# Transposing the residual unnormalised during the output projection, with the first two query blocks and six gate chunks moved

## The chip, the cores and the metric

The kernel runs on one core of a Trainium2 chip. The metric is the device time of one execution in microseconds (us), as a median of several runs. One core has TensorE (PE, matmuls; PEld is its weight load), VectorE (DVE), ScalarE (ACT), GpSimd (POOL) and SyncE (SP), which work in parallel, each in the order of its own queue. In this program SP issues nearly all large loads, and POOL the small transfers and the stores.

## The reference

One decoder layer on 256 tokens of width 2048, all in float32: a modulated norm, an input projection, sparse attention and retention side by side, an output projection with a gated residual, a second modulated norm, and a retrieval of experts (PEER) with a gated residual.

```python
mod = (c_act @ w_ada[l] + b_ada[l]).reshape(B, 6, 1, D)
shift1, scale1, gate1, shift2, scale2, gate2 = jnp.moveaxis(mod, 1, 0)
...
x = x + gate1 * (jnp.concatenate([o_nsa, o_ret], axis=-1) @ w_out[l])
h2 = rmsnorm(x, g_norm_ffn[l]) * (1.0 + scale2) + shift2
x = x + gate2 * peer_ffn(h2, peer_w_q[l], peer_sub_keys[l], peer_u[l], peer_v[l])
return rmsnorm(x, g_norm_final)
```

In `peer_ffn`, `q = h2 @ w_q` gives 8 heads x 2 halves of 128 numbers per token, that is 16 query blocks of 128 columns. Each is scored against 128 keys, the best 16 of each half are paired, and the best 16 of the pairs are the experts. Each token then needs `gelu(h2 . u)` and a sum of rows of `v` for its experts only.

## The kernel before, in words

Weights come in chunks of 128x2048 numbers, 1 MB each. `load` (L146) issues one on SP into a slot `raw`. `split_to` (L153) makes two reduced-precision halves of it: ACT casts the high part (`whi`, L157), and VectorE subtracts it from the original for the low part (`wlo`, L158). A product is then three matmuls (high x high, high x low, low x high). The activations stand likewise as `hh` and `hl`, the two halves of the tile `act`.

**The six modulation vectors** are 6 x 16 chunks of `adaT`. `ada_chunk` (L195) loads one and multiplies it by the row of c on VectorE with a running sum (L198). `background(pace)` (L327) interleaves them with other work from the list `todo`: at each call it adds `PACE[pace]` to a credit and takes as many chunks as the credit has whole numbers. Vector 5 is gate 2; it is needed only at the end of the program. Six of its 16 chunks stand at the end of `todo` (`LATE = 6`), ten are done in the query stage.

**Output projection.** `n_tile(q, "woutN", ...)` (L442) is called for four column blocks q, each with four chunks of weights and 96 matmuls into `psN`. Its result is multiplied by gate 1 (`xg`, L716) and added to the residual `x2` (L717). ACT sums the squares (L719), and POOL stores `x2` (L720). `x2` and `xT` are two views of the same memory.

**The turn.** When the last block is done, the reciprocal root-mean-square `rc` of each token is taken (L723), `x2` is multiplied by it (`xn`, L728), 32 transposes go into `psX` (L733), ACT and VectorE by turns add scale and shift into `xT` (L737 and L739), ACT casts `hh` (L740) and VectorE makes `hl` (L741).

**Query stage.** A second pool of slots opens (five `raw`, three `whi`, two `wlo`), over memory of the front. First come the loads of the keys (`skT`) and of the first two weight chunks `wqT`. `t_blocks` (L227) makes the first two query blocks side by side: for each of 16 steps k and each block a matmul of 128x512 with the high weights on both halves of `act` (L236) and one of 128x256 with the low weights on `hh` (L237). Fourteen single blocks follow. Each block is summed into `pq` (ACT L245, VectorE L246), scored (`pss`, L1089), and its top 16 are found on VectorE (L1071 to L1075); block 2 is split into a tile `pair` of its own, so that its split can be done early. In the first ten rounds an `ada_chunk` of gate 2 is done with `crow2`, a copy of the row of c that POOL loads (L1133). From the scores come candidates, the picks and the indices for gathers.

**Activation and value halves.** `u_half` (L1238) goes through 64 chunks of `u`, each 16 matmuls into `psU` (L1062); beside it one-hot matrices `pg` mark the experts. `v_group` multiplies with the chunks of `v`. The order is u half 0, v group 0, u half 1, v group 1. In u half 1 the chunks use slots of `raw` and three of `whi`, one after another in a ring (`set_ring`, L129). Before u half 0, gate 2 is finished into a row (`row5`, L1272 to L1279).

What sets the order: a scheduler places the instructions of each engine by program order and by `tc.high_priority`; loads wait for the slot that they reuse.

Of the kernel before, what the change touches and what calls it, by code (L numbers as in the profile page):

```python
# [30 lines left out]
PACE = dict(A=2, C=0.5, B=0.8, pair=1.5, tile=1.4, head=1.4, out=0.75)  # L31
LATE = 6
# [83 lines left out]
def body(ctx, tc, a, out, dbg=None, stop=None):  # L116
# [110 lines left out]
    def t_blocks(pool, src_chunks, tags=("A", "A"), parts=1, dst=None):  # L227

        if dst:
            split_to(load(src_chunks[0]), *dst, parts)  # L230
        w = [dst] if dst else [split(load(c), parts=parts) for c in src_chunks]
        ps = [pool.tile([P, 2, S], F32, name="psA", tag=t) for _, t in zip(w, tags)]
        for k in range(KB):
            sl = slice(k * P, (k + 1) * P)
            for p_, (hi, lo) in zip(ps, w):
                nc.tensor.matmul(p_, hi[:, sl], act[:, k], start=k == 0, stop=False, skip_group_check=True)  # L236
                nc.tensor.matmul(p_[:, 1, :], lo[:, sl], hh[:, k, :], start=False, stop=k == KB - 1, skip_group_check=True)  # L237
        return ps

    def t_block(pool, src_chunk, tag="A", **kw):  # L240
        return t_blocks(pool, [src_chunk], (tag,), **kw)[0]
# [36 lines left out]
    with ExitStack() as fctx:  # L278
# [43 lines left out]

        todo = [(j, k) for k in range(KB) for j in (1, 0)] + [(j, k) for j in (2, 4, 3) for k in range(KB)] + [(5, k) for k in range(LATE)]

# [68 lines left out]
        for k in range(KB):  # L393
# [3 lines left out]
            if len(todo) > 46 + LATE:  # L397
                background("B")
# [322 lines left out]
        xn = fp.tile([P, 2, D], F32, name="xn", tag="oT")  # L721
        with tc.high_priority(offset=100):
            rc = token_rstd(fp, ss, 2, "rc")  # L723
        for q in range(4):
            sl = slice(q * 512, (q + 1) * 512)
            with tc.high_priority(offset=(4 - q) * 40):
                for tt in range(2):
                    nc.vector.tensor_scalar(xn[:, tt, sl], x2[:, tt, sl], rc[:, tt:tt + 1], None, op0=OP.mult)  # L728
        for k in range(KB):
            with tc.high_priority(offset=(KB - k) * 10):  # L730
                ps = pp.tile([P, 2, P], F32, name="psX", tag="TO"[k % 2])
                for tt in range(2):
                    nc.tensor.transpose(ps[:, tt, :], xn[:, tt, k * P:(k + 1) * P], ident)  # L733
                t = xT[:, k, :]
                ps = ps.rearrange("p t s -> p (t s)")
                if k % 2:
                    nc.vector.tensor_scalar(t, ps, scol[:, 1, k:k + 1], modc[:, 3, k:k + 1], op0=OP.mult, op1=OP.add)  # L737
                else:
                    nc.scalar.activation(t, ps, AF.Identity, bias=modc[:, 3, k:k + 1], scale=scol[:, 1, k:k + 1])  # L739
                nc.scalar.copy(hh[:, k, :], t)  # L740
                nc.vector.tensor_sub(hl[:, k, :], t, hh[:, k, :].bitcast(F32))  # L741


    with ExitStack() as gctx:
# [338 lines left out]
        wq = lambda i: a["wqT"][i].rearrange("p k e -> p (k e)")  # L1083
# [188 lines left out]
        nc.vector.tensor_add(modc[:, 5, :], modc[:, 5, :], b_col[:, 5, :])  # L1272
        nc.vector.tensor_scalar(modc[:, 5, :], modc[:, 5, :], 1.0 / GSC, None, op0=OP.mult)
        ps = up.tile([P, 512], F32, name="psh", tag=bank("S"))
        nc.tensor.transpose(ps[0:KB, 0:P], modc[:, 5, :], ident)
        r5 = gp_.tile([KB, P], F32, name="row5t", tag="ge", bufs=3)
        nc.scalar.copy(r5, ps[0:KB, 0:P])
        row5 = dram.tile([1, D], F32, name="row5")
        nc.gpsimd.dma_start(row5.rearrange("o (k p) -> (o k) p", p=P), r5)  # L1279
# [36 lines left out]
```

## Time and profile before

| | |
|---|---|
| median of 3 runs | 1909.55 us (1908.13 to 1912.08) |
| profiled execution | 1904.08 us |
| span of its trace | 1902.3 us |
| mean granted TensorE clock | 0.982 |
| bytes moved | 652.91 MB, mean 343 GB/s |

The span reaches from the first to the last instruction; 1.8 us of the profiled execution lie around it. Times in rows are microseconds from the start of the span, "mean ns" is that of one instruction. A matmul's time is pipelined: successive ones overlap, so the distance of their starts is the better measure. "x16" in a row stands for 16 instructions. In brackets or after the last bar stands the time that the engine was idle just before, and what ended it. Names are those of the program: `psN` and `psA` are PSUM tiles of the output projection and of the query blocks, and a row "psN L452 <- DVE wlo L158" is a wait of TensorE for a split.

### The profile page before, as it was taken

How to read it: one execution, taken by the hardware profiler on the slowest of the kernel's cores; microseconds unless marked ns; L12 is line 12 of the kernel's file. 1: busy time of each engine (PE TensorE's matmuls, PEld its weight loads, DVE VectorE, ACT ScalarE, POOL GpSimd, SP SyncE). 2: the span in 40 equal slices, each digit the busy share in tenths (PEclk: the TensorE clock that was granted, in tenths of full speed). 3: DMA queues.
4: the chain of work that ended last, by engine and by line, in shares of the span. 5: the costliest groups of instructions: out<-in, count | busy, mean ns of one | idle time of the engine just before them, and what ended most of it. 6: DMA issues, size and time to landing. Idle time of an engine off the chain costs nothing.

```text
span 1902.3 us, 28433 instructions
## 1 busy us (share of the span) xinstructions
PE 1811.7 (95%) x11303; PEld 1585.4 (83%) x11303; DVE 1477.1 (78%) x2247; ACT 697.5 (37%) x1191; POOL 370.8 (19%) x256
## 2 busy tenths in 40 slices
PE   5899899999988999999999999999999999999995
PEld 3799878798776899999997777779999997777773
DVE  7878887889768999677478999984455567888875
ACT  3344453545425421021035555541111114555542
POOL 1000000012000012211124333331111114544210
PEclk9999999999998999999999999999999999999998
DMA  8989888989778879989989999989999989999981
GB/s 337 371 314 351 319 331 245 346 280 345 265 258 343 297 284 361 425 351 360 373 327 378 420 413 414 414 322 426 365 361 368 351 318 391 404 387 387 384 298 44
DMA packets 94471, 652.91 MB, mean 343 GB/s; under 512 B 11409, under 2 KB 11617, under 8 KB 18433
## 3 DMA queue, kind: packets, MB, share of 16 engines
q1 hardware_dynamic: 66818, 467.78, 64.8%
q0 software_dynamic: 27520, 183.32, 24.2%
q8 instruction: 89, 1.46, 0.3%
q14 instruction: 44, 0.36, 0.1%
HBM read 644.97 MB, written 4.22 MB: 341 GB/s over the span
## 4 chain that ended last, share of the span: by engine, by line
PE 72%; DVE 12%; DMA 11%; issue 3%; ACT 1%; POOL 0%; SPq 0%; ACTq 0%; POOLq 0%; DVEq 0%
PE acc L964 31%; PE psU L1062 25%; DMA raw<-in_adaT 7%; PE psN L452 5%; DVE wlo L158 3%; PE psA L236 2%; PE psD L353 2%; DVE raw L198 2%; DMA raw<-in_winB 1%; PE bkC L353 1%; PE psA L237 1%; PE pg L1047 1%; ACT whi L157 1%; DMA raw<-in_winA 1%; DVE s L844 1%
## 5 line engine op out<-in xcount | busy, mean ns | idle before, releaser
L1062 PE MATMUL psU<-xT,raw 128*128 128x160 f32 x4096 | 571.1, 301 | 4.0 <-ACT ge L1067 2.5
L1062 PEld LDWEIGHTS psU<-xT,raw 128*128 128x128 f32 x4096 | 559.9, 191 | 5.0 <-ACT ge L1067 2.6
L964 PE MATMUL acc<-whi,cc 128*128 128x512 f32 x1512 | 367.8, 391 | 0.0
L947 DVE TENSOR_TENSOR wlo<-raw,whi 128x2048 fp32r<-128x2048 f32 x126 | 288.3, 2288 | 72.3 <-issue 59.3
L964 PEld LDWEIGHTS acc<-whi,cc 128*128 128x128 f32 x1512 | 283.9, 188 | 68.8 <-issue 0.2
L964 PE MATMUL acc<-wlo,cc 128*128 128x512 f32 x1008 | 254.2, 393 | 2.4 <-DVE wlo L947 2.4
L198 DVE SCALAR_TENSOR_TENSOR raw<-raw,crow 128x2048 f32<-128x2048 f32 x96 | 219.3, 2287 | 38.1 <-DMA raw<-in_adaT 37.7
L946 ACT CAST whi<-raw 128x2048 fp32r<-128x2048 f32 x126 | 240.7, 1911 | 0.0
L157 ACT CAST whi<-raw 128x2048 fp32r<-128x2048 f32 (+2 forms) x89 | 161.0, 1813 | 216.5 <-DMA raw<-in_winA 35.8
L964 PEld LDWEIGHTS acc<-wlo,cc 128*128 128x128 f32 x1008 | 163.0, 162 | 63.7 <-DVE wlo L947 2.9
L158 DVE TENSOR_TENSOR wlo<-raw,whi 128x2048 fp32r<-128x2048 f32 (+2 forms) x89 | 192.6, 2168 | 28.9 <-ACT whi L157 28.2
L452 PE MATMUL psN<-whi,act 128*128 128x512 f32 x512 | 169.4, 407 | 0.3 <-ACT whi L157 0.3
L1068 DVE TENSOR_TENSOR X<-X,ge 128x160 f32<-128x160 f32 (+19 forms) x94 | 25.9, 277 | 164.5 <-ACT ge L1067 164.4
L1064 ACT ACTIVATE X<-psU 128x160 f32<-128x160 f32 (+19 forms) x102 | 25.5, 251 | 322.5 <-PE psU L1062 322.5
L452 PEld LDWEIGHTS psN<-whi,act 128*128 128x128 f32 x512 | 97.5, 192 | 24.7 <-issue 1.7
L452 PE MATMUL psN<-wlo,act 128*128 128x512 f32 x256 | 104.3, 408 | 7.5 <-DVE wlo L158 7.5
L941 ACT CAST cc<-X 128x192 fp32r<-128x192 f32 x128 | 44.7, 353 | 142.3 <-PE acc L964 141.4
L803 POOL DMA_INDIRECT rows<-in_urow,sx x32 | 69.3, 2165 | 135.4 <-DVE rows L844 122.0
L236 PE MATMUL psA<-act,whi 128*128 128x512 f32 x240 | 88.5, 409 | 3.1 <-ACT whi L157 3.1
L803 POOL DMA_INDIRECT xT<-in_v,sx x21 | 62.8, 2992 | 107.6 <-DVE cc L942 63.3
L948 ACT CAST cc<-cc 128x64 fp32r<-128x64 f32 x128 | 31.1, 243 | 132.4 <-DVE cc L942 132.3
L353 PE MATMUL psD<-act,whi 128*128 128x256 f32 x384 | 76.4, 296 | 3.0 <-ACT whi L157 3.0
(350 smaller groups left out, 2551.7 us busy)
## 6 DMA issues: line engine op xcount, KB each, us to landing
raw<-in_u SPq DMA_DIRECT2D x128, 1024.0 KB, 8.9
raw<-in_v SPq DMA_DIRECT2D x128, 1024.0 KB, 9.4
raw<-in_adaT SPq DMA_DIRECT2D x96, 1024.0 KB, 6.5
raw<-in_winN SPq DMA_DIRECT2D x16, 1024.0 KB, 6.9
raw<-in_woutN SPq DMA_DIRECT2D x16, 1024.0 KB, 6.1
raw<-in_wqT SPq DMA_DIRECT2D x16, 1024.0 KB, 6.7
raw<-in_winB SPq DMA_DIRECT2D x16, 832.0 KB, 6.7
raw<-in_winD SPq DMA_DIRECT2D x12, 1024.0 KB, 6.6
```

The costliest lines, as they stand in the source:

```text
L157: nc.scalar.copy(hi[:, sl], r[:, sl])
L158: nc.vector.tensor_sub(lo[:, sl], r[:, sl], hi[:, sl].bitcast(F32))
L198: nc.vector.scalar_tensor_tensor(r, r, 1.0, crow, op0=OP.mult, op1=OP.mult, accum_out=modc[:, j, k:k + 1])
L236: nc.tensor.matmul(p_, hi[:, sl], act[:, k], start=k == 0, stop=False, skip_group_check=True)
L353: nc.tensor.matmul(bank[:, b, :], x[:, w], y[:, k, :], start=k == k0 and n == 0 and first, stop=k == k1 - 1 and n == 2, skip_group_check=True)
L452: nc.tensor.matmul(ps[tt], x[:, k, ts_], y[:, w], start=k == 0 and j == 0, stop=k == KB - 1 and j == 2)
L803: pin(nc.gpsimd.indirect_dma_start(out=r, out_offset=None, in_=src, in_offset=bass.IndirectOffsetOnAxis(ap=o, axis=0)))
L941: inorder(nc.scalar.copy(ch, xb(j)))
L946: inorder(nc.scalar.copy(hi, r))
L947: nc.vector.tensor_sub(lo, r, hi.bitcast(F32))
L964: nc.tensor.matmul(acc[c][0:m], x, w[:, c[1] * 512:(c[1] + 1) * 512], start=jj == 0 and n == 0, stop=jj == HALF - 1 and n == 2 - c[0], ski ...
L1062: nc.tensor.matmul(ps, w[:, k * P:(k + 1) * P], xT[:, k, 0:TU], start=k == 0, stop=k == KB - 1)
```

## The change

It has three parts.

1. **Transposing without the norm.** A function `turn(q)` transposes the four 128-column pieces of block q of `x2` as they are, during the next block of the output projection, and ACT applies the scale of the norm (`scol`) into a new tile `yT`. When the last block is done, `rc` is taken as before, and `turn(3)` follows; `rc` is spread over the partitions by a diagonal (`dg`) and a matmul with ones (`psr2`); four multiplications on VectorE scale `yT`. ACT adds the shift on the way to `hh`, VectorE makes `hl` in one step, and ACT writes `xT` apart.
2. **First two query blocks in the front.** Their weights are loaded after the last woutN chunk into slots of the front, split in two parts each, and multiplied before the second pool opens. The sums go to DRAM (`q01`) and come back as `pq` in the query stage. There, the weights of block 2 are loaded first, then `skT`, then those of block 3; later loads stand two blocks ahead.
3. **Gate 2.** `todo` ends with vector 3 (`LATE` is gone, the pace "out" is 0.7), the query stage does chunks 0 to 9, and `gate2(j)` in u half 1 does chunks 10 to 15 at j = 4, 12, 20, 28, 36, 44. The row of c for them is loaded at j = 1 into a `whi` slot (so the ring has two instead of three), and `row5` is made at j = 53.

```diff
-PACE = dict(A=2, C=0.5, B=0.8, pair=1.5, tile=1.4, head=1.4, out=0.75)
-LATE = 6
+PACE = dict(A=2, C=0.5, B=0.8, pair=1.5, tile=1.4, head=1.4, out=0.7)
+EARLY5 = 10
...
+        yT = fp.tile([P, KB, S], F32, name="yT", tag="oT")
+
+        def turn(q):
+
+            for k in range(4 * q, 4 * q + 4):
+                ps = pp.tile([P, 2, P], F32, name="psX", tag="TO"[k % 2])
+                for tt in range(2):
+                    nc.tensor.transpose(ps[:, tt, :], x2[:, tt, k * P:(k + 1) * P], ident)
+                nc.scalar.activation(yT[:, k, :], ps.rearrange("p t s -> p (t s)"), AF.Copy, scale=scol[:, 1, k:k + 1])
+
...
+            if q > 0:
+                turn(q - 1)
             if q == 3:
                 background(len(todo))
+                wq01 = [load(wq_src(i)) for i in range(2)]
...
+        with tc.high_priority(offset=200):
+            rc = token_rstd(fp, ss, 2, "rc")
+            turn(3)
+            dg = fp.tile([P, S], F32, name="dg2", tag="pr", bufs=3)
+            for tt in range(2):
+                nc.vector.tensor_scalar(dg[:, tt * P:(tt + 1) * P], ident, rc[:, tt:tt + 1], None, op0=OP.mult)
+            psr = pp.tile([P, S], F32, name="psr2", tag="A")
+            nc.tensor.matmul(psr, ones, dg, start=True, stop=True)
         with tc.high_priority(offset=100):
-            rc = token_rstd(fp, ss, 2, "rc")
+            wq01 = [split(r, parts=2) for r in wq01]
         for q in range(4):
...
+            sl = slice(4 * q, 4 * q + 4)
+            nc.vector.tensor_mul(yT[:, sl, :], yT[:, sl, :], psr[:, None, :].to_broadcast([P, 4, S]))
+            for k in range(4 * q, 4 * q + 4):
+                b = modc[:, 3, k:k + 1]
+                nc.scalar.activation(hh[:, k, :], yT[:, k, :], AF.Identity, bias=b)
+                nc.vector.scalar_tensor_tensor(hl[:, k, :], yT[:, k, :], b, hh[:, k, :].bitcast(F32), op0=OP.add, op1=OP.subtract)
+        first = t_blocks(pp, wq01, ("A", "T"))
+        for k in (0, 1, 2, 3, 4, 5, 8, 9, 10, 11, 12, 13, 6, 7, 14, 15):
+            nc.scalar.activation(xT[:, k, :], yT[:, k, :], AF.Identity, bias=modc[:, 3, k:k + 1])
+        q01 = dram.tile([2, P, S], F32, name="q01")
+        for i in range(2):
+            q = fp.tile([P, S], F32, name="q01s", tag="nal", bufs=4)
+            summed(first[i], q)
+            nc.gpsimd.dma_start(q01[i], q)
...
-        sk = load(a["skT"].rearrange("p k e -> p (k e)"))
...
+        raws = [load(wq_src(2))]
+        sk = load(a["skT"].rearrange("p k e -> p (k e)"))
+        raws.append(load(wq_src(3)))
...
-        first = t_blocks(up, [wq(0), wq(1)], (bank("A"), bank("A")), 2)
...
+            if i < 2:
+                nc.gpsimd.dma_start(q, q01[i])
+            else:
+                r = raws.pop(0)
+                if i == 2:
+                    split_to(r, *early)
+                ps, = t_blocks(up, [early if i == 2 else split(r)], (qbank(i),))
+                if i < 14:
+                    raws.append(load(wq_src(i + 2)))
+                summed(ps, q)
             pend.append((i, q))
-            if i < KB - LATE:
-                ada_chunk(5, LATE + i, crow2)
+            if i < EARLY5:
+                ada_chunk(5, i, crow2)
...
-                        set_ring(late, raw=5, whi=3)
+                        set_ring(late, raw=5, whi=2)
...
                 if hf:
+                    gate2(j)
...
+            if j == 1:
+                crow3.append(chunk_tile("crow3", F32, "whi"))
+                row_load(crow3[0], rowc)
+            if 4 <= j < 52 and j % 8 == 4:
+                ada_chunk(5, EARLY5 + j // 8, crow3[0])
```

The order of the instructions, as the two programs have it, shows what the diff alone does not. Each row is one instruction: line, operation, output and inputs, size, and the engines or DMA queues whose semaphores it waits for (DMAHW: landing of a load from SP; DMASW: of a transfer from POOL).

First SP's loads at the end of the output projection and the start of the query stage, before:

```order
L148 DMA raw<-in_adaT 128x2048 [waits DVE_49]
L148 DMA raw<-in_skT 128x2048 [waits DMAHW6_49,DMAHW3_49,DVE_49]
L148 DMA raw<-in_wqT 128x2048 [waits PE_49]
L148 DMA raw<-in_wqT 128x2048 [waits DMAHW1_49,DMAHW0_49]
L148 DMA raw<-in_adaT 128x2048
L148 DMA raw<-in_adaT 128x2048 [waits DMAHW2_49]
L148 DMA raw<-in_wqT 128x2048 [waits DMAHW7_49,DVE_49]
```

And with the change:

```order
L148 DMA raw<-in_woutN 128x2048 [waits DMAHW7_49,DMAHW3_49,DVE_49]
L148 DMA raw<-in_wqT 128x2048 [waits DMAHW4_49,DVE_49]
L148 DMA raw<-in_wqT 128x2048 [waits DMAHW5_49,DVE_49]
L148 DMA raw<-in_wqT 128x2048 [waits DMAHW2_49,DMAHW1_49,DVE_49]
L148 DMA raw<-in_skT 128x2048 [waits PE_49]
L148 DMA raw<-in_wqT 128x2048 [waits DMAHW6_49]
L148 DMA raw<-in_adaT 128x2048 [waits DMAHW7_49]
L148 DMA raw<-in_adaT 128x2048 [waits DMAHW0_49]
L148 DMA raw<-in_wqT 128x2048 [waits DMAHW2_49,DVE_49]
```

The wait of `skT` for PE is for the last matmul of the first two query blocks, whose weights stood in the memory of its slot; before, the wait of the first `wqT` for PE was for the last psN matmul. The output projection now has 8 loads of `adaT` among its woutN loads instead of 14.

Second, VectorE from the splits of the first query weights to the split of block 3, before (`pair` is block 2, L246 the sums `pq` of blocks 0 and 1):

```order
L741 TENSOR_TENSOR act<-xT,act 128x256 [waits Activation_49] x6
L158 TENSOR_TENSOR wlo<-raw,whi 128x1024 [waits DMAHW7_49,Activation_49]
L158 TENSOR_TENSOR wlo<-raw,whi 128x1024 [waits Activation_49]
L158 TENSOR_TENSOR wlo<-raw,whi 128x1024 [waits DMAHW0_49,Activation_49]
L158 TENSOR_TENSOR wlo<-raw,whi 128x1024 [waits Activation_49]
L198 SCALAR_TENSOR_TENSOR raw,modc<-raw,crow_4910 128x2048 [waits DMAHW1_49,DMASW3_49]
L198 SCALAR_TENSOR_TENSOR raw,modc<-raw,crow_4910 128x2048 [waits DMAHW2_49]
L158 TENSOR_TENSOR pair_4888<-raw,pair_4888 128x2048 [waits DMAHW3_49,Activation_49]
L246 TENSOR_TENSOR pq<-pq,psA 128x256 [waits Activation_49] x2
L198 SCALAR_TENSOR_TENSOR raw,modc<-raw,crow_4910 128x2048 [waits DMAHW4_49,DVE_49]
L158 TENSOR_TENSOR wlo<-raw,whi 128x2048 [waits DMAHW5_49,Activation_49]
```

And with the change, from the diagonal (L736) on, with the scaling of `yT` (L743) and `hl` (L747); ahead of these rows stand the splits of the first query weights and the two steps to `rc`:

```order
L736 TENSOR_SCALAR dg_4821<-small,rc 128x128 [waits Pool_49]
L736 TENSOR_SCALAR dg_4821<-small,rc 128x128
L743 TENSOR_TENSOR yT<-yT,psr_4824 128x1024 [waits PE_49]
L743 TENSOR_TENSOR yT<-yT,psr_4824 128x1024 x2
L743 TENSOR_TENSOR yT<-yT,psr_4824 128x1024 [waits Activation_49]
L747 SCALAR_TENSOR_TENSOR act<-yT,modc,act 128x256 [waits Activation_49] x16
L243 TENSOR_TENSOR q01s<-q01s,psA 128x256 [waits Activation_49] x2
L158 TENSOR_TENSOR pair_4978<-raw,pair_4978 128x2048 [waits DMAHW2_49,Activation_49]
L158 TENSOR_TENSOR wlo<-raw,whi 128x2048 [waits DMAHW4_49,Activation_49]
L243 TENSOR_TENSOR pq<-pq,psA 128x256 [waits Activation_49]
L198 SCALAR_TENSOR_TENSOR raw,modc<-raw,crow_5004 128x2048 [waits DMAHW5_49,DMASW5_49]
L198 SCALAR_TENSOR_TENSOR raw,modc<-raw,crow_5004 128x2048 [waits DMAHW6_49]
```

The two gate chunks that stood ahead of the split of block 2 now stand behind the sum of block 2, and the first of them waits for a transfer of POOL (`crow2`); the split of block 2 stands behind the sums of blocks 0 and 1. The split of block 4 follows eight rows behind the second of them.

Third, ACT at the same place, before and, in the second piece, with the change, where L750 writes the last of `xT` and L242 copies out of psA:

```order
L157 CAST pair_4888<-raw 128x2048 [waits DMAHW3_49,PE_49]
L245 COPY pq<-psA 128x256 [waits PE_49] x2
L157 CAST whi<-raw 128x2048 [waits DMAHW5_49]
L157 CAST whi<-raw 128x2048 [waits DMAHW7_49,DVE_49]
L245 COPY pq<-psA 128x256 [waits PE_49]
```

```order
L750 ACTIVATE xT<-yT,modc 128x256 [waits DMASW0_49]
L750 ACTIVATE xT<-yT,modc 128x256
L242 COPY q01s<-psA 128x256 [waits PE_49] x2
L157 CAST pair_4978<-raw 128x2048 [waits DMAHW2_49,DVE_49,Activation_49]
L157 CAST whi<-raw 128x2048 [waits DMAHW4_49]
L242 COPY pq<-psA 128x256 [waits PE_49]
```

The cast of block 2 (`pair`) stood ahead of the first two copies out of psA; now it stands behind them.

On POOL, the load of `crow2` stood behind two small constants (`ident`, `iota`); now the two stores of `q01` stand ahead of these.

More of the change, by code (lines that the diff above doesn't have):

```diff
@@ L225, in body, with t_blocks @@
     hh, hl = act[:, :, 0, :], act[:, :, 1, :]
[L227 to L232, printed above, removed]
+    def t_blocks(pool, w, tags):
+        ps = [pool.tile([P, 2, S], F32, name="psA", tag=t) for t in tags]
         for k in range(KB):
@@ L238, in t_blocks, with wq_src @@
         return ps
-    def t_block(pool, src_chunk, tag="A", **kw):
-        return t_blocks(pool, [src_chunk], (tag,), **kw)[0]
+    def wq_src(i):
+        return a["wqT"][i].rearrange("p k e -> p (k e)")
     def summed(ps, dst, n=S):
@@ L321, in body @@
             normalise(xT[:, k:k + 4, :], xT[:, k:k + 4, :], rrow)
-        todo = [(j, k) for k in range(KB) for j in (1, 0)] + [(j, k) for j in (2, 4, 3) for k in range(KB)] + [(5, k) for k in range(LATE)]
+        todo = [(j, k) for k in range(KB) for j in (1, 0)] + [(j, k) for j in (2, 4, 3) for k in range(KB)]
         credit = [0.0]
@@ L361, in row_in @@
         def row_in(k):
-            while len(todo) > 80 + LATE - 2 * (k + 1):
+            while len(todo) > 80 - 2 * (k + 1):
                 background(1)
@@ L396, in body @@
                 row_in(k)
-            if len(todo) > 46 + LATE:
+            if len(todo) > 46:
                 background("B")
@@ L720, in body @@
                     nc.gpsimd.dma_start(x2d[:, tt, sl], x2[:, tt, sl])
-        xn = fp.tile([P, 2, D], F32, name="xn", tag="oT")
+        with tc.high_priority(offset=200):
[6 more added lines that the diff above has]
+            nc.tensor.matmul(psr, ones, dg, start=True, stop=True)
@@ L722, in body @@
         with tc.high_priority(offset=100):
-            rc = token_rstd(fp, ss, 2, "rc")
+            wq01 = [split(r, parts=2) for r in wq01]
         for q in range(4):
[L725 to L741, printed above, removed]
@@ L1133, in body @@
         row_load(crow2, rowc)
-        first = t_blocks(up, [wq(0), wq(1)], (bank("A"), bank("A")), 2)
+        qbank = lambda i: f"b{(6, 7, 2, 3)[i % 4]}"
         for i in range(16):
-            ps = first[i] if i < 2 else t_block(up, wq(i), bank("A"), dst=early if i == 2 else None)
             q = tk.tile([P, S], F32, name="pq", bufs=3)
-            summed(ps, q)
+            if i < 2:
[8 more added lines that the diff above has]
+                summed(ps, q)
             pend.append((i, q))
-            if i < KB - LATE:
-                ada_chunk(5, LATE + i, crow2)
+            if i < EARLY5:
+                ada_chunk(5, i, crow2)
             if 4 <= i < 8:
@@ L1269, in u_half, with gate2 @@
                     sparse(j in STEPS["u0"])
[L1272 to L1277, printed above, removed]
-        row5 = dram.tile([1, D], F32, name="row5")
-        nc.gpsimd.dma_start(row5.rearrange("o (k p) -> (o k) p", p=P), r5)
+        row5 = dram.tile([1, D], F32, name="row5")
+        crow3 = []
+        def gate2(j):
+            if j == 1:
[3 more added lines that the diff above has]
+                ada_chunk(5, EARLY5 + j // 8, crow3[0])
+            elif j == 53:
+                nc.vector.tensor_add(modc[:, 5, :], modc[:, 5, :], b_col[:, 5, :])
+                nc.vector.tensor_scalar(modc[:, 5, :], modc[:, 5, :], 1.0 / GSC, None, op0=OP.mult)
+                ps = up.tile([P, 512], F32, name="psh", tag=bank("S"))
+                nc.tensor.transpose(ps[0:KB, 0:P], modc[:, 5, :], ident)
+                r = gp_.tile([KB, P], F32, name="row5t", tag="ge", bufs=3)
+                nc.scalar.copy(r, ps[0:KB, 0:P])
+                nc.gpsimd.dma_start(row5.rearrange("o (k p) -> (o k) p", p=P), r)
         for _ in range(2):
```

1 line of the change is left out of this document (removed).

## Prediction

> **What bounds the kernel now.** The page's totals come first, then its group of gate chunks.
>
> ```profile
> span 1902.3 us, 28433 instructions
> PE 1811.7 (95%) x11303; PEld 1585.4 (83%) x11303; DVE 1477.1 (78%) x2247; ACT 697.5 (37%) x1191; POOL 370.8 (19%) x256
> ...
> L198 DVE SCALAR_TENSOR_TENSOR raw<-raw,crow 128x2048 f32<-128x2048 f32 x96 | 219.3, 2287 | 38.1 <-DMA raw<-in_adaT 37.7
> ```
>
> TensorE is busy for 95%, so a gain can only come from the other 5%. A gate chunk (L198) costs VectorE 2.287 us, and VectorE stood idle 38.1 us ahead of such chunks, waiting for their loads. Where does TensorE wait? Its waits from 470 to 570 us (the output projection), and those from 586 to 995 us:
>
> ```profile
> PE psN L452 <- DVE wlo L158: 6.5, 3, 2.6
> ```
>
> ```profile
> PE psU L1062 <- ACT ge L1067: 2.5, 1, 2.5
> ...
> PE ptr L1190 <- DVE ex L1128: 0.3, 1, 0.3
> ```
>
> The first stretch has a few waits, the longest on VectorE's splits. The second has six groups of them, of which the first and the last stand here, 6.0 us together in 409. So the change can win only in the output projection and in the turn after it; later it can only lose. The stretches of these stages (busy us of each engine, then granted clock, DMA share, GB/s), and the psN matmuls alone:
>
> ```profile
> 516.00:568.60 52.60, 49.92 (x206) 39.13 (x204) 38.36 (x32) 15.96 (x15) 2.16 (x4) 0.97 0.74 263
> 568.60:600.40 31.80, 21.20 (x97) 16.46 (x97) 26.42 (x48) 16.80 (x36) 4.01 (x6) 0.79 0.86 324
> 600.40:686.40 86.00, 86.00 (x515) 75.98 (x516) 85.28 (x283) 35.27 (x43) 2.10 (x4) 1.00 0.80 292
> ```
>
> ```profile
> 464.00:516.00 52.00, 46.77 (x179) 34.84 (x179) 1.38 (x2) 0.14 (x1) 0.93 0.79 287
> 516.00:568.60 52.60, 49.92 (x206) 39.13 (x204) 3.44 (x5) 0.00 (x0) 0.97 0.74 263
> ```
>
> Two readings follow. The turn (568.6 to 600.4) leaves TensorE idle for 10.6 of 31.8 us. In the query stage (600.4 to 686.4) TensorE and VectorE are both full, 86.00 and 85.28 of 86: whatever comes late to VectorE there is late for good.
>
> **The output projection.** The chain of waits shows the loss, the timeline its end:
>
> ```profile
> 495.35 0.23 PE psT L512 x2
> ...
> 525.79 8.63 DMA raw<-in_adaT
> ...
> 536.81 2.21 DVE wlo L158
> 539.07 28.80 PE psN L452 x115
> ```
>
> ```profile
> 567.93 0.39 PE L452 MATMUL psN<-wlo,act 128*128 128x512 f32 x1
> 568.16 0.39 PE L452 MATMUL psN<-whi,act 128*128 128x512 f32 x1
> ```
>
> VectorE works in the order of its queue: at 525.79 it waits 8.63 us for a gate chunk, and the woutN split behind it comes late. Unhindered, psN matmuls start every 0.23 us. The second half thus lost 52.6 - 206 x 0.23 = 5.2 us, the first about 52.0 - 179 x 0.23 = 10.8, some of it to other matmuls. Of 14 chunk loads in this stage 8 stay. The order of SP's loads is unchanged up to the third woutN chunk; 5 of 6 remain ahead of the eighth and 3 of 8 behind it. So I take 5/8 of 5.2 = 3.3 us off the second half, and 0.4 off the first, where at most 10.8/6 = 1.8 can go: -3.7, ends 0 and -7.0. The change adds 24 transposes here (three calls of turn), each 0.115 us by the row of psT (two in 0.23): +2.8, or 0 if they fall into the remaining stalls. Their 12 ACT evictions are hidden: ACT is busy 15.96 of 52.6 us. Sum: the last psN matmul ends 0.9 us sooner, ends -7.0 and +2.8. I call that moment T; before it is 568.16 + 0.39 = 568.55.
>
> **The turn.** Before, with the rows of the timeline that price the new steps:
>
> ```profile
> 571.49 0.16 DVE L214 TENSOR_REDUCE rc<-ss 128x2 f32<-128x8 f32 x1 [0.85 <-ACT sq L719]
> 572.68 3.26 DVE L728 TENSOR_SCALAR xn<-xT,rc 128x512 f32<-128x512 f32 x8 [0.83 <-POOL rc L220]
> 573.31 5.16 PE L733 MATMUL psX<-small,xn 128*128 128x128 f32 x22 [4.76 <-DVE xn L728]
> 574.07 0.80 POOL L209 DMA_DIRECT2D crow<-rowc  x1
> 584.82 0.79 PE L236 MATMUL psA<-act,whi 128*128 128x512 f32 x1 [3.14 <-ACT whi L157]
> 585.02 4.63 DVE L158 TENSOR_TENSOR wlo<-raw,whi 128x1024 fp32r<-128x1024 f32 x4
> 588.60 0.63 PE L236 MATMUL psA<-act,whi 128*128 128x512 f32 x1
> 591.16 0.42 PE L236 MATMUL psA<-act,whi 128*128 128x512 f32 x1
> 592.28 1.91 ACT L157 CAST pair<-raw 128x2048 fp32r<-128x2048 f32 x1 [4.67 <-DMA raw<-in_wqT]
> 594.69 0.39 PE L236 MATMUL psA<-act,whi 128*128 128x512 f32 x1
> 595.04 0.40 PE L236 MATMUL psA<-act,whi 128*128 128x512 f32 x1
> 599.48 0.73 ACT L245 COPY pq<-psA 128x256 f32<-128x256 f32 x2 [5.29 <-PE psA L237]
> 600.36 0.50 PE L236 MATMUL psA<-act,pair 128*128 128x512 f32 x1 [0.56 <-DVE pq L246]
> ```
>
> Before, rc starts at T+2.9. Now two halves of a wlo split (4.63/4 = 1.16 each) stand ahead of it on VectorE: T+5.3. From rc to its first use took 1.19 us: T+6.5. The diagonal and the ones-matmul have no row; from xn to its first transpose took 0.63, so I estimate 0.9: T+7.4. Four 128x1024 multiplies at 1.16 each all stand ahead of the first hl: T+12.0, with the first hl T+12.4. ACT writes hh and xT in between, some 25 casts of about 0.4 us, done by T+20, ahead of TensorE. TensorE then has 32 pairs of matmuls: at 0.64 us (588.60 to 591.16 is four of them) while its clock is low, at 0.35 (594.69 to 595.04) after. Before, the slow ones lasted from 584.82 to 591.16, the time of ten; 10 x 0.64 + 22 x 0.35 = 14.1, so both blocks end at T+26.5. Before, it was 599.48 (the first pq copy waits for it), T+30.9: 4.4 us won.
>
> That gain is not kept. In ACT's new order the two q01s copies (0.73) and then the cast of block 2 (1.91) follow the last of these matmuls, and the split (2.2) follows on VectorE: T+31.3, against 600.36 = T+31.8 before. Block 2 ends at T+31.3 + 16 x 0.35 = T+36.9.
>
> The Trainium skill, "TensorE: Matmul & The Clock Gate", Part 1, says that the clock falls to half after an idle window of about 3.4 us. TensorE would idle T+26.5 to T+31.3; by that rule ten pairs of block 2 cost 0.29 more each, 2.9 in all, and block 2 would end at T+39.8, which the waits below mostly hide (+0.7 at most). The trace shows the slow pairs after an idle stretch of 4.76 us, but not which idle stretch caused them.
>
> **The query stage.** The skT load now stands behind wq2 in SP's queue and waits for the last matmul of the first two blocks; wq3 and two gate chunks stand behind it; before, skT was loaded ahead of the first query block. On POOL, crow2 stands behind the q01 stores. Transfers around the turn (KB, median us to landing), and what follows on VectorE, ACT and TensorE:
>
> ```profile
> raw<-in_wqT SPq DMA_DIRECT2D x5, 1024.0 KB, 5.9
> ...
> crow<-rowc POOLq DMA_DIRECT2D x1, 1024.0 KB, 12.9
> ```
>
> ```profile
> 607.20 2.29 DVE L158 TENSOR_TENSOR wlo<-raw,whi 128x2048 fp32r<-128x2048 f32 x1
> 612.55 0.36 ACT L245 COPY pq<-psA 128x256 f32<-128x256 f32 x1
> 686.60 0.28 PE L237 MATMUL psA<-act,wlo 128*128 128x256 f32 x1
> ```
>
> Four loads of 1 MB from T+26.5: the first lands 5.9 later, the others 2.5 apart (1.05 MB at the 425 GB/s shown below): skT T+32.4, wq3 T+34.9, chunks T+37.4 and T+39.9. Block 3's cast and split end at T+39.1, pq of block 2 at T+39.5. Next on VectorE stand two gate chunks, which need crow2: issued near T+29.8 (both q01 stores and two constants, at some 0.7 us each, from T+27), it lands at T+42.7 if it takes 12.9 us as before, at T+35.7 if 5.9 like a weight chunk. So the two chunks, at 2.2 each, end at T+44.3 (waiting for their own loads) or T+47.2, and behind seven small top-k steps and a sum (2 us) the split of block 4 ends at T+48.5 or T+51.4. Before, that split was done at T+41, and TensorE began block 4 when block 3 ended, at 612.55 = T+44.0. TensorE is 4.5 or 7.4 us late. After that VectorE has 11 splits, 8 chunks and eleven top-k rounds, about 66 us until block 15, and TensorE 12 blocks in 74.3 (T+44.0 to T+118.3 before): TensorE no longer waits, but nothing is regained. Term: +6, ends +1.5 (loads and crow2 land as soon as skT did, T+31) and +7.4.
>
> The gather indices come late by as much or a little more; VectorE waited 10.9 us for the first pg of the first activation half, which covers it:
>
> ```profile
> DVE X L1052 <- PE pg L1047: 10.9, 1, 10.9
> ```
>
> **Second activation half.** Its start, its end, and SP's waits:
>
> ```profile
> 1283.00:1310.00 27.00, 27.00 (x211) 26.85 (x210) 10.48 (x14) 3.58 (x10) 4.69 (x5) 1.00 1.01 426
> 1310.00:1340.00 30.00, 30.00 (x247) 29.92 (x246) 13.83 (x25) 4.42 (x20) 4.15 (x3) 1.00 1.01 425
> 1466.00:1576.00 110.00, 110.00 (x944) 109.63 (x943) 64.26 (x95) 19.46 (x65) 19.69 (x14) 1.00 0.86 331
> ```
>
> ```profile
> SPq L148 <- PE psU L1062: 271.0, 61, 9.1
> ```
>
> Seven more MB (six chunks and the row), 7 x 2.5 = 17 us of full transfer. The first three fall into the full stretch and push the u loads back by 7.4 us. But SP waits for TensorE to free slots: the loads run a ring ahead, 7 slots of about 4.6 us now instead of 8, and land in 9. VectorE's six chunks are 13.7 us where it is busy 10.48 of 27 or 64.26 of 110. I take 0, ends 0 and +2.
>
> **The sum** against the profiled execution: -0.9 + 6.0 + 0 = +5.1, 1904.1 + 5.1 = 1909.2 us. The median of the runs shown is 5.5 us above that execution: 1909.55 + 5.1 = 1914.7.
>
> **The rivals.**
> Faster: the stalls of the output projection go to the low end, -7.0, the transposes fall into what is left of them, and in the query stage the loads land early (+1.5): -5.5, 1904.1. For it speaks the 38.1 us in which VectorE waits for gate chunks; against it that 5 of 6 remain in the first half, and that skT waits in the program as built. It decides if T moves by more than the query stage loses.
> The same: T at -5, the query stage at +4.5: -0.5, 1909.1. For it: both are within the bounds.
> Slower still: the second activation half has no room. If the 7.4 us of pushed loads reach TensorE, 1914.7 + 7.4 = 1922.1. For it the share of 1.01, against it that TensorE never waits for a load there. It decides if the ring's lead falls under the landing time.
> I exclude that the change does not do what it says: its loads and transposes stand in the order.
>
> **Chances.** Forecast 0.44, slower still 0.08, the same 0.26, faster 0.22. This kernel's measurement can tell about 0.2%, 3.8 us. So slower 0.52, same 0.26, faster 0.22. The range reaches from the faster case to the upper ends of the three terms (1909.55 + 2.8 + 7.4 + 2 = 1921.8): 1903 to 1921.8.
>
> **What would show it.** In the changed profile: T near 567.7 us; the first two blocks ending near T+26; an idle TensorE until T+31; the skT load issued only then; VectorE waiting for crow2 or the chunks near T+39; block 4 starting near T+50; psA ending near T+124. I am wrong if T comes before 563, if TensorE does not wait between blocks 3 and 4, or if it waits for loads in the second activation half.

## The result, and the profile after

The changed kernel takes 1918.41 us in the median (9 runs, 1910.6 to 1921.38), the kernel before 1908.13 (9 runs, 1898.45 to 1912.08). The ratio is 1.0059, 95% interval 1.0038 to 1.0079: by the ratio 11.2 us slower (the medians differ by 10.3), by the interval 7 to 15. The profiled execution is the one of 1918.41 us.

The head of the page with the change, and its group of gate chunks:

```profile
span 1916.6 us, 28444 instructions
PE 1816.4 (95%) x11305; PEld 1589.2 (83%) x11305; DVE 1475.8 (77%) x2237; ACT 707.8 (37%) x1215; POOL 357.0 (19%) x261
...
L198 DVE SCALAR_TENSOR_TENSOR raw<-raw,crow 128x2048 f32<-128x2048 f32 x96 | 219.3, 2286 | 41.2 <-DMA raw<-in_adaT 36.3
```

The work is as it was. VectorE has 1.3 us less of it, and 14.3 us more of span to do it in. The idle time ahead of gate chunks is no smaller: 36.3 us behind their loads, where it was 37.7, although six of them left the front.

Where the time came from shows in landmarks that both traces have: the last gate of the retention (the tile sg), the first `xg`, the last psN matmul. Each row gives the first and the last start of its group; before and, below, with the change:

```profile
L631 ACT ACTIVATE sg<-psN x4: 598/601/602, 350.8 to 463.5; 128x512 f32<-128x512 f32 x4
L716 DVE TENSOR_TENSOR xg<-psN,g x8: 682/686/692, 498.0 to 569.2; 128x512 f32<-128x512 f32 x8
L452 PE MATMUL psN<-whi,act x512: 387/396/632, 239.8 to 568.2; 128*128 128x512 f32 x171
```

```profile
L628 ACT ACTIVATE sg<-psN x4: 597/600/601, 349.0 to 466.9; 128x512 f32<-128x512 f32 x4
L726 DVE TENSOR_TENSOR xg<-psN,g x8: 681/686/692, 513.0 to 575.5; 128x512 f32<-128x512 f32 x8
L449 PE MATMUL psN<-whi,act x512: 387/396/632, 239.6 to 574.4; 128*128 128x512 f32 x171
```

The last gate starts 3.4 us later with the change, though nothing that bears on it was edited. In the ten later traces below it starts anywhere from 460.8 to 472.6, so differences of some us up to that point are those of single executions. From it on, column block 0 is done after 513.0 - 466.9 = 46.1 us instead of 34.5, and the last psN matmul starts after 107.5 instead of 104.7. Block 0 lost 11.6 us, and the rest of the output projection won 8.8.

The next stages go by the same landmarks: last psN matmul to last psA matmul 127.8 us (118.4 before), from there to the first matmul of the value group 304.7 (304.4), to the last psU matmul 586.1 (584.6), to the last matmul of the second value group 293.4 (296.5). The differences, +2.8, +9.4, +0.3, +1.5 and -3.1, make +10.9.

What happened in block 0 stands in the chain of waits with the change:

```profile
490.50 2.29 DVE raw L198 x2
...
492.82 6.71 DMA raw<-in_adaT
...
501.93 2.21 DVE wlo L158
...
504.19 8.34 PE psN L449 x28
...
512.55 1.91 ACT whi L157
...
514.49 2.30 DVE wlo L158
```

VectorE did one gate chunk at 490.5, and only then was there a slot for the next chunk's load (492.82). That next chunk stood ahead of a woutN split in VectorE's queue, so TensorE waited for the split until 504.19. VectorE's waits for gate chunks from the last gate to the first `xg` (us in total, times, longest), before (463.5 to 498 us) and with the change (466.9 to 513):

```profile
DVE raw L198 <- DMA raw<-in_adaT: 3.0, 2, 2.2
```

```profile
DVE raw L198 <- DMA raw<-in_adaT: 15.5, 4, 6.2
```

That is 12.5 us more, enough for all of the 11.6 that block 0 lost.

The turn and the query stage with the change, in rows picked from the timelines of the engines:

```profile
586.99 0.79 PE L233 MATMUL psA<-act,whi 128*128 128x512 f32 x1 [5.10 <-DVE act L747]
599.66 0.33 SPq L148 DMA_DIRECT2D raw<-in_skT  x1
602.01 0.49 PE L233 MATMUL psA<-act,pair 128*128 128x512 f32 x1 [2.26 <-ACT pair L157]
602.75 0.55 POOL L209 DMA_DIRECT2D crow<-rowc  x1
604.33 0.58 PE L234 MATMUL psA<-act,pair 128*128 128x256 f32 x1 [1.83 <-DVE pair L158]
604.71 0.63 PE L233 MATMUL psA<-act,pair 128*128 128x512 f32 x1
605.35 0.63 PE L233 MATMUL psA<-act,pair 128*128 128x512 f32 x1
610.39 2.29 DVE L158 TENSOR_TENSOR wlo<-raw,whi 128x2048 fp32r<-128x2048 f32 x1 [6.11 <-ACT whi L157]
612.79 0.37 ACT L242 COPY pq<-psA 128x256 f32<-128x256 f32 x1 [2.43 <-PE psA L234]
618.42 2.29 DVE L198 SCALAR_TENSOR_TENSOR raw<-raw,crow 128x2048 f32<-128x2048 f32 x1 [4.80 <-DMA crow<-rowc]
620.39 0.37 ACT L1106 COPY tsc<-pss 128x256 f32<-128x256 f32 x1 [7.23 <-PE pss L1104]
620.93 1.91 ACT L157 CAST whi<-raw 128x2048 fp32r<-128x2048 f32 x1
624.82 2.27 DVE L158 TENSOR_TENSOR wlo<-raw,whi 128x2048 fp32r<-128x2048 f32 x1
627.14 0.38 PE L234 MATMUL psA<-act,wlo 128*128 128x256 f32 x1 [0.76 <-DVE wlo L158]
```

With T = 574.4 + 0.4 = 574.8: the first query matmul at T+12.2, the skT load at T+24.9, block 2 in earnest at T+29.5 and done at T+38.0, its first ten pairs 0.64 us apart. VectorE waits 4.8 us for crow2, which lands 15.7 us after its issue. The split of block 4 ends at T+52.3, and TensorE starts block 4 with it. That is 8.3 us later than before, and the stage ends 9.4 later.

### The profile page after: what moved, and what is told of

It is laid out like the page before. It is cut to its first block, busy times and chain, and to the rows that moved or that the text cites. A ratio compares the mean times of both kernels' runs of the same rounds, so it can differ in the third digit from the quotient of the medians.

```text
span 1916.6 us, 28444 instructions
## 1 busy us (share of the span) xinstructions
PE 1816.4 (95%) x11305; PEld 1589.2 (83%) x11305; DVE 1475.8 (77%) x2237; ACT 707.8 (37%) x1215; POOL 357.0 (19%) x261
## 4 chain that ended last, share of the span: by engine, by line
PE 69%; DVE 13%; DMA 9%; issue 6%; ACT 2%; POOL 1%; SPq 0%; ACTq 0%; POOLq 0%; DVEq 0%
PE acc L978 30%; PE psU L1076 26%; PE psN L449 5%; DMA raw<-in_adaT 4%; DVE wlo L158 4%; DVE raw L198 2%; PE psD L350 1%; PE bkC L350 1%; DMA raw<-in_winA 1%; ACT whi L157 1%; DMA raw<-in_winB 1%; PE pg L1061 1%; DMA raw<-in_winD 1%; DMA pq<-q 1%; PE pT L545 1%
## 5 line engine op out<-in xcount | busy, mean ns | idle before, releaser
L198 DVE SCALAR_TENSOR_TENSOR raw<-raw,crow 128x2048 f32<-128x2048 f32 x96 | 219.3, 2286 | 41.2 <-DMA raw<-in_adaT 36.3
L955 ACT CAST cc<-X 128x192 fp32r<-128x192 f32 x128 | 44.7, 353 | 137.6 <-PE acc L978 134.4
```

The source lines that it names most:

```text
L198: nc.vector.scalar_tensor_tensor(r, r, 1.0, crow, op0=OP.mult, op1=OP.mult, accum_out=modc[:, j, k:k + 1])
L955: inorder(nc.scalar.copy(ch, xb(j)))
```

## The experiments

Ten kernels ran on the chip. The table shows each stage by the landmarks above, as a difference to the kernel before in us, their sum, and the measured ratio with its 95% interval. "Out" is the output projection, "query" goes from the last psN to the last psA matmul, "u0" and "v0+u1" and "v1" are the later stages.

| kernel | out | query | u0 | v0+u1 | v1 | sum | ratio |
|---|---|---|---|---|---|---|---|
| the change | +2.8 | +9.4 | +0.3 | +1.5 | -3.1 | +10.9 | 1.0059 (1.0038 to 1.0079) |
| e1: change, pace 0.75 | -2.3 | +10.5 | +0.1 | +0.2 | -0.6 | +7.9 | 1.0037 (1.0016 to 1.0058) |
| e2: change, chunks later | +2.1 | +3.2 | +1.7 | +1.0 | -3.1 | +4.9 | 1.0025 (1.0005 to 1.0045) |
| e3: before, part 3 | -4.5 | +4.8 | +1.9 | +0.8 | +0.9 | +3.9 | 1.0020 (0.9999 to 1.0040) |
| e5: before, part 1 | +2.4 | +8.8 | +2.3 | 0.0 | +0.2 | +13.7 | 1.0079 (1.0052 to 1.0106) |
| e6: e1 and e2 | -4.6 | +4.1 | +2.4 | +1.1 | -3.2 | -0.2 | 0.9993 (0.9972 to 1.0014) |
| e7: e6, skT on POOL | -3.6 | +0.6 | +1.6 | +1.3 | -3.2 | -3.3 | 0.9971 (0.9950 to 0.9992) |
| e9: e3, chunks later | -4.3 | +0.2 | +5.4 | +0.7 | -0.6 | +1.4 | 0.9990 (0.9972 to 1.0009) |
| e12: change, crow2 on SP | +1.4 | +8.8 | +0.8 | +1.6 | -3.2 | +9.4 | 1.0059 (1.0039 to 1.0079) |
| e13: e7, gap filled | -2.3 | -0.2 | +1.5 | +1.2 | -3.2 | -3.0 | 0.9977 (0.9959 to 0.9995) |
| e14: before, pace 0.7 | +5.0 | +4.2 | +3.4 | +0.1 | -2.3 | +10.4 | 1.0076 (1.0051 to 1.0101) |

One trace stands behind each row; each sum lies within the interval of its ratio. e1, e6, e7 and e13 have the same output projection and show -2.3 to -4.6, so differences of 2 us in one cell mean nothing.

**The pace.** e1 is the changed kernel with one number put back:

```diff
-PACE = dict(A=2, C=0.5, B=0.8, pair=1.5, tile=1.4, head=1.4, out=0.7)
+PACE = dict(A=2, C=0.5, B=0.8, pair=1.5, tile=1.4, head=1.4, out=0.75)
```

> The changed kernel with the pace of the output projection back at 0.75, and nothing else. Theory (the pace shifted two gate chunks next to each other ahead of the end of column block 0, where VectorE waits 6 us twice for their loads): the last psN matmul ends near 568 us instead of 574.8, the query stage stays 9 us late, and the time falls by 5 to 7 us against the changed kernel, to about +5 us against the kernel before. Rival (the transposes between the psN matmuls are what delays the output projection): the last psN matmul stays near 574 us and the time stays about 11 us above the kernel before.

Measured: 1.0037, some 7 us where about 5 was expected. Its landmarks:

```profile
L628 ACT ACTIVATE sg<-psN x4: 597/599/602, 348.1 to 463.7; 128x512 f32<-128x512 f32 x4
L726 DVE TENSOR_TENSOR xg<-psN,g x8: 681/682/692, 498.2 to 567.2; 128x512 f32<-128x512 f32 x8
```

Block 0 is done 34.5 us after the last gate, as before the change. The output projection is 5.1 us shorter than in the changed kernel, and the query stage stays late. e14 does the reverse: the kernel before with this pace alone.

```diff
-PACE = dict(A=2, C=0.5, B=0.8, pair=1.5, tile=1.4, head=1.4, out=0.75)
+PACE = dict(A=2, C=0.5, B=0.8, pair=1.5, tile=1.4, head=1.4, out=0.7)
```

> The kernel before with pace 0.7 instead of 0.75 in the output projection, and nothing else. Theory (this pace alone puts two gate chunks next to each other in VectorE's queue ahead of the end of column block 0): the first xg comes 10 to 12 us later after the last gate of retention than before (45 instead of 34.5), the output projection is 3 to 6 us longer, and the time 3 to 9 us above the kernel before, as the order in the query stage moves too. Rival (it was the pace together with the transposes): the output projection stays at 104.7 us.

Measured: 1.0076, that is 14.5 us and more than the 3 to 9 expected. Its landmarks:

```profile
L631 ACT ACTIVATE sg<-psN x4: 598/600/601, 351.1 to 468.0; 128x512 f32<-128x512 f32 x4
L716 DVE TENSOR_TENSOR xg<-psN,g x8: 683/684/692, 513.3 to 578.8; 128x512 f32<-128x512 f32 x8
```

45.3 us to the first `xg`, as in the changed kernel. With both runs it is shown: the pace makes the output projection about 5 us longer, with the transposes or without. (The four traces of the changed kernel at 0.75 have 33.2 to 34.5 us up to the first `xg`, the three at 0.7 have 44.7 to 46.1.) VectorE's queue says how. At 0.75, gate chunks and splits alternate up to the first `xg`; at 0.7 there stand, in this order, two splits, two chunks, one split, one chunk. Fewer chunks per call brought two of them next to each other. The query stage of e14, 4.2 us longer, has the slip that e3 shows below: the split of block 2 (611.63) stands behind the sums of blocks 0 and 1 (609.83).

**The transposes and the gate chunks apart.** e5 is the kernel before with part 1 alone: `turn`, the ones-matmul and the scaling, without the early query blocks; e3 is the kernel before with part 3 alone at pace 0.75. In short, of e5 and then of e3:

```diff
-        xn = fp.tile([P, 2, D], F32, name="xn", tag="oT")
+        yT = fp.tile([P, KB, S], F32, name="yT", tag="oT")
...
+            if q > 0:
+                turn(q - 1)
...
+            turn(3)
```

```diff
-LATE = 6
+LATE, EARLY5 = 0, 10
...
-            if i < KB - LATE:
-                ada_chunk(5, LATE + i, crow2)
+            if i < EARLY5:
+                ada_chunk(5, i, crow2)
...
-                        set_ring(late, raw=5, whi=3)
+                        set_ring(late, raw=5, whi=2)
...
+                    gate2(j)
```

> The kernel before with part 1 alone: the residual transposed unnormalised during the output projection, scaled by the norm afterwards. Theory: 24 transposes cost up to 2.8 us in the output projection, the turn to the first query matmul is 2 to 4 us shorter: -2 to +1 us against the kernel before. Rival (the transposes stall the psN matmuls, and ACT's xT copies lengthen the turn): +3 to +6 us.

> The kernel before with part 3 alone: six gate chunks in the second activation half (with the row in a slot of whi), none of gate 2 in the output projection; pace 0.75. Theory: the output projection ends 3 to 5 us sooner, the query stage is unchanged, the second activation half costs 0 to 2: the time is 1 to 5 us below the kernel before. Rival (the second activation half has no room for 7 MB more): the half is 5 to 7 us longer and the time is 1 to 4 us above the kernel before.

Measured: 1.0079 for part 1, 1.0020 for part 3. In the output projection both did what was expected, +2.4 for 24 transposes and -4.5 for six chunks less; the second activation half takes 0.8 more with part 3. Both lost in the query stage, which neither theory had. In e5 the first query matmul comes at 21.5 us after the last psN matmul instead of 16.6. It waits for ACT, whose casts of the first query weights stand behind its last writes of `xT`:

```profile
593.14 2.88 ACT L749 ACTIVATE xT<-yT,modc 128x256 f32<-128x256 f32 x7
595.93 3.87 ACT L157 CAST whi<-raw 128x1024 fp32r<-128x1024 f32 x4
597.01 0.79 PE L236 MATMUL psA<-act,whi 128*128 128x512 f32 x1 [15.15 <-ACT whi L157]
```

This half of the rival came true, though the time is +15 us by the ratio, more than its +3 to +6; this delay is 4.9 of it. In the changed kernel, where part 2 loads these weights early, ACT has cast them by 576.8, before the steps of the turn: part 1 leans on part 2. In e3 the order of the queues changed where nothing had been edited. Before, the split of block 2 starts at 594.22, ahead of the sums of blocks 0 and 1; in e3 it stands behind them:

```profile
601.09 0.76 DVE L246 TENSOR_TENSOR pq<-pq,psA 128x256 f32<-128x256 f32 x2 [6.13 <-ACT pq L245]
603.23 2.29 DVE L158 TENSOR_TENSOR pair<-raw,pair 128x2048 fp32r<-128x2048 f32 x1 [1.38 <-ACT pair L157]
```

VectorE waited 6.13 us for the first two blocks with that split undone behind the wait. e9 tests it: e3 with the ten chunks of the query stage two rounds later.

```diff
-            if i < EARLY5:
-                ada_chunk(5, i, crow2)
+            if 2 <= i < EARLY5 + 2:
+                ada_chunk(5, i - 2, crow2)
```

> The kernel before with part 3 alone, and the ten gate chunks of the query stage two rounds later, which puts the split of block 2 back ahead of the sums of blocks 0 and 1. Theory (part 3 gains 4 to 5 us in the output projection, and lost it again in the query stage because the order of VectorE's and ACT's queues there changed): output projection 4 to 5 us shorter than before, query stage as before or 1 us shorter, second activation half 1 longer: -3 to -5 us against the kernel before. Rival (the query stage of part 3 alone was late for another reason): the stage stays 4 to 5 us longer, 0 to +4.

Measured: 0.9990, not to be told from the kernel before, where 3 to 5 us less was expected. The query stage is back (+0.2), as expected, and the output projection keeps its 4.3; but the first activation half is 5.4 longer in this trace, where TensorE waits 4.5 and 2.4 us for ACT. Why it does was not tried.

**The query stage of the change.** e2 is the changed kernel with the same edit as e9, at pace 0.7.

> The changed kernel with the ten gate chunks of the query stage two rounds later (rounds 2 to 11 instead of 0 to 9); the skT load and the rest stay. Theory (VectorE waits for the row crow2 and then does two chunks ahead of the split of block 4): that split ends near 52 - 9 = 43 us after the last psN matmul, psA ends 4 to 6 us sooner, and the time falls by 4 to 6 us against the changed kernel, to +5 to +7 us against the kernel before. Rival (the blocked skT load and the loads behind it are what delays block 4): no change, +11 us.

Measured: 1.0025; the query stage is 6.2 us shorter. VectorE around block 3 in e2:

```profile
605.53 2.29 DVE L158 TENSOR_TENSOR wlo<-raw,whi 128x2048 fp32r<-128x2048 f32 x1 [7.60 <-ACT whi L157]
608.17 2.29 DVE L158 TENSOR_TENSOR wlo<-raw,whi 128x2048 fp32r<-128x2048 f32 x1 [0.34 <-ACT whi L157]
610.38 0.41 DVE L243 TENSOR_TENSOR pq<-pq,psA 128x256 f32<-128x256 f32 x1
```

The splits of blocks 3 and 4 stand together, both ahead of the sum of block 2. So two things changed at once: the chunks no longer wait for crow2 there, and the split of block 4 no longer stands behind anything that waits for TensorE. e12 was to change the first alone, in the changed kernel:

```diff
-        row_load(crow2, rowc)
+        nc.sync.dma_start(crow2, bass.AP(tensor=rowc.tensor, offset=rowc.offset, ap=[[0, P], [1, D]]))
```

> The changed kernel with one load moved: the row crow2 is issued by SP (behind skT and the third query weight) instead of POOL, where it stood behind the two stores of q01 and two constants. Theory (VectorE's wait for crow2 is what makes block 4 late): crow2 lands near 36 us after the last psN matmul instead of 43.6, the last query matmul comes 3 to 4 us sooner after the last psN matmul (124 instead of 127.8), the time falls by 3 to 4 us against the changed kernel, to +7 to +8 us against the kernel before. Rival (the two gate chunks in front of the split are enough, whatever crow2 does): the last query matmul stays at 127 to 128, +10 to +11.

Measured: 1.0059, the same as the change, as the rival had it. VectorE no longer waits for crow2, and another wait has taken its place. VectorE's waits in e12 from 590 to 700 us, the third and the fourth, and rows picked from its timeline:

```profile
DVE V L1085 <- ACT tsc L1106: 1.7, 1, 1.7
DVE raw L198 <- DMA raw<-in_adaT: 1.5, 1, 1.5
```

```profile
623.09 0.49 DVE L1085 MAX8 V<-tsc 128x8 f32<-128x128 f32 x2 [1.72 <-ACT tsc L1106]
623.50 0.41 DVE L243 TENSOR_TENSOR pq<-pq,psA 128x256 f32<-128x256 f32 x1
624.86 0.49 DVE L1088 MAX8 V<-twk 128x8 f32<-128x128 f32 x2
625.51 2.29 DVE L158 TENSOR_TENSOR wlo<-raw,whi 128x2048 fp32r<-128x2048 f32 x1
```

The split of block 4 (625.51) stands behind the first top-k step and behind the sum of block 3 (623.50), and both need what TensorE makes with and after block 3. So this split cannot start before TensorE has run out of blocks, whenever crow2 lands. ACT's cast for it stands behind two copies of the same kind as well and ends at 625.13. Before, the splits ran one or two blocks ahead of the sums, as the order of the queue shows.

But e12 also made block 3 late, so it does not show that crow2 cost nothing. With one more load on SP, the weights of block 3 were cast at 610.77 (T+35.6; in the change at 608.46, T+33.7), and TensorE waited for their split:

```profile
610.77 1.90 ACT L157 CAST whi<-raw 128x2048 fp32r<-128x2048 f32 x1 [7.92 <-DMA raw<-in_wqT]
615.05 0.57 PE L234 MATMUL psA<-act,wlo 128*128 128x256 f32 x1 [1.82 <-DVE wlo L158]
```

The last matmul of block 3 starts at T+46.7 in e12 and at T+43.2 in the change. From there to the end of the split of block 4 it is 5.9 us in e12 and 9.0 in the change. So the wait for crow2 held that split for about 3 us, which e12 lost again in block 3; the other 5.9 us stand without it, by the order of the queues.

**Both, and the blocked load.** e6 has the pace of e1 and the chunks of e2. e7 adds one line: skT goes into its slot by POOL, so that SP's queue does not stand behind its wait.

```diff
-        sk = load(a["skT"].rearrange("p k e -> p (k e)"))
+        sk = raw_tile()
+        nc.gpsimd.dma_start(sk, a["skT"].rearrange("p k e -> p (k e)"))
```

> The changed kernel with both: pace 0.75 in the output projection, and the ten gate chunks of the query stage two rounds later. Theory (the two losses are separate and add up): output projection 2 us shorter than before, last query matmul 3 us later after the last psN matmul than before, second activation half 1 us longer: +1 to +3 us against the kernel before. Rival (the one loss hides the other, as both make VectorE wait): no better than with either alone, +5 to +7.

> As the run with pace 0.75 and the later chunks, and the skT load issued by POOL instead of SP, so that the third query weight and the gate chunks no longer stand behind its wait. Theory (with crow2 off the path, the blocked loads are what is left: TensorE waits 2 us for block 3): last query matmul 2 to 3 us sooner, -1 to +1 us against the kernel before. Rival (the loads were never late for anything, or skT on POOL comes late for the scores): no change or slower, +2 or more.

Measured: 0.9993 and 0.9971, some 3 to 5 us better than expected, of which the shorter second value half is the largest part. The losses of pace and order add up (by the stages e6 is 11.1 us shorter than the change, e1 3.0 and e2 6.0), and the blocked loads cost another 3.5 us of the query stage (122.5 to 119.0) once the split is out of the way; in the changed kernel itself block 3 was split at 612.7, when block 2 was done at 612.8, so there they cost nothing. By its interval e7 is 1.5 to 9.5 us faster than the kernel before. It is the fastest of these versions, with e13.

**The low clock.** e13 is e7 with 18 matmuls in the gap ahead of block 2, whose result nothing reads:

```diff
+        fill = pp.tile([P, 512], F32, name="fill", tag="S")
+        for i in range(18):
+            nc.tensor.matmul(fill, hh[:, KB - 1, 0:P], act[:, KB - 1], start=i == 0, stop=i == 17)
```

> As the run with pace 0.75, the later chunks and skT on POOL, with 18 matmuls of 128x512 put behind the first two query blocks, whose result nothing uses; they keep TensorE busy for 4 us until the weights of block 2 are there. Theory (the low clock in block 2, 0.63 us for a pair of matmuls instead of 0.35, comes from the idle gap ahead of it and costs 16 times 0.28): block 2 takes 6 instead of 8 to 10 us, the last query matmul comes 2 to 4 us sooner, -5 to -9 us against the kernel before. Rival (the gap has nothing to do with it, or VectorE's splits set the pace of the next blocks anyway): the last query matmul stays, -3 to -5 us or, if the 18 matmuls delay block 2, less.

The matmuls of block 2 with the high weights, in the change and in e13 (ns shortest/median/longest, first and last start):

```profile
L233 PE MATMUL psA<-act,pair x16: 392/628/628, 602.0 to 612.2; 128*128 128x512 f32 x16
```

```profile
L233 PE MATMUL psA<-act,pair x16: 389/392/402, 600.9 to 606.7; 128*128 128x512 f32 x16
```

All 16 run fast when the gap is filled: the gap is what slows them. The granted clock shows it too (stretch, its length, busy us of PE, PEld, DVE, ACT and POOL, then the clock, DMA share, GB/s), in the change, in e7 and in e13:

```profile
599.80:604.30 4.50, 0.49 (x1) 0.19 (x1) 3.06 (x3) 2.15 (x3) 2.74 (x5) 0.93 0.79 259
604.30:610.50 6.20, 6.17 (x20) 5.29 (x21) 0.11 (x1) 1.90 (x1) 1.10 (x2) 0.50 1.03 398
610.50:618.30 7.80, 7.80 (x45) 6.59 (x44) 2.61 (x2) 0.37 (x1) 0.00 (x0) 1.00 1.01 423
```

```profile
604.40:607.90 3.50, 3.46 (x11) 2.98 (x12) 3.50 (x2) 1.26 (x1) 0.61 (x2) 0.52 0.91 349
```

```profile
601.50:607.00 5.50, 5.48 (x31) 4.79 (x32) 4.37 (x2) 1.26 (x1) 0.59 (x2) 1.00 0.94 381
```

In the change ten pairs ran at the low clock, in e7 only five, after the same gap. So in e7 there were only 5 x 0.29 = 1.4 us to gain, and not 16 x 0.28 as the theory had it. Block 2 ends 0.9 us sooner after the last psN matmul than in e7 and the stage 0.8 sooner; the ratio, 0.9977, can't be told from that of e7.

## Why the prediction was right or wrong

The direction was right, and the time lies in the range, but the loss is twice the forecast: +11.2 us instead of +5.1. (The low end of the range, 1903, does not follow from the faster case, which comes to 1904.1; it decides nothing here.)

- **The output projection: wrong, -0.9 forecast, +2.8 found.** The step that failed is "0.4 off the first half". I took from the order that SP's loads there were nearly unchanged, and they were; VectorE's queue was not, and it sets the time. A row or two of chunks and splits changed places, and the pace alone is worth about +5 us (e1, e14). The other two terms were good: -3.7 for the six chunks against -4.5 (e3) and -4.3 (e9), +2.8 for the transposes against +2.4 (e5, one trace, hardly more than the spread of this column).
- **The turn: right.** First query matmul at T+12.2 (forecast T+12.4), first two blocks done at T+24.7 (T+26.5), then an idle TensorE and the loads issued only then.
- **The clock in block 2: the Trainium skill was nearer than I.** I let block 2 run at full clock, to T+36.9, and its rule ("TensorE: Matmul & The Clock Gate", Part 1), with the ten slow pairs of the turn before, gave T+39.8. The trace agrees with the rule: the granted clock was 0.50 for ten pairs, and e13 shows that the gap causes it. The idle window of 3.4 us itself is not tested: the gap of 4.5 us had one matmul in it, and in e7 five pairs were slow after the same gap. Block 2 was done at T+38.0, as it started 1.8 us sooner than I had it.
- **The query stage: right in place, too small, and its cause only in part.** I had the split of block 4 end at T+48.5 or T+51.4 and took the middle; crow2 took 15.7 us to land instead of 12.9, and the split ended at T+52.3. The stage lost 9.4 instead of 6. I named the two chunks and crow2 as what holds the split, and in the changed kernel they do: the "seven small steps and a sum (2 us)" took just these 2 us behind them. But without the wait for crow2 5.9 of 9.0 us stay (e12), since the same queue holds the sum of block 3 and a top-k step, which wait for TensorE, ahead of the split. My forecast priced these by their durations alone. The blocked skT load, which I put at the head of this part, decided nothing in the changed kernel.
- **The second activation half: right.** +0.2 to +1.6 in the traces with part 3, within 0 to +2; TensorE does not wait for loads there.
- **Not foreseen: the second value half is 3.1 us shorter.** TensorE's longest wait for a split in it falls from 2.4 to 0.6 us, and in its first 24 us the granted clock is 1.00 instead of 0.93. e14, which moves nothing there, shows -2.3 as well, e1 only -0.6. What decides it is left open.
- **The rivals.** Faster: its -7.0 for the stalls was too much (part 3 at pace 0.75 gains 4.5), and its transposes were not free; the pace took the rest. e7 reaches its time, 5.5 us faster by the ratio, but not by its sum: 3.2 us of that come from the second value half, which no case had. The same: it needed T 5 us sooner, and the output projection became longer. Slower by the second activation half: excluded by the traces.

## What to carry to other kernels

In an in-order queue, price an instruction by what it waits for, not by how long it takes: a 0.4 us sum ahead of a split ends the lookahead of a whole pipeline. When a scheduler writes the order, a change of one number can move neighbours far from the edit, so print the order of the engine that bounds each stage, before and after, and look there for two loads' consumers side by side and for a producer that has slipped behind a consumer. And look in the trace of an experiment whether only the thing to be tested has moved: e12 moved one load, and with it block 3. Undoing the three slips (a pace, ten chunks, one load) turned 0.59% slower into 0.29% faster.

## What the runs showed of the hardware

The row of c, 1 MB read by all partitions from one row, took 12.9 us to land before and 15.7 with the change, when four other loads of 1 MB were issued in the 4 us ahead of it; weight chunks of the same size took 5.9. In e7, with one load of 1 MB issued in the 4 us ahead of it, it took 9.6. And after a gap of 4.5 us with one matmul in it, TensorE's granted clock was 0.50 for 6.2 us in the changed kernel, and ten pairs ran 0.64 us apart instead of 0.35; after the turn before it was 6.3 us, in e7 after the same gap only about 3.4 us and five pairs. With the gap filled the clock stayed at 1.00.
